# Hymba-style block on one core: the first x and weight transfers on ScalarE's queue, the selector copied on GpSimd, one block-sum transfer placed later

## The chip, the core and the metric

The kernel runs on one core of one Trainium2 chip. The metric is the device time of one execution in microseconds; of three runs of the kernel before the median is 900.09 us (900.05 to 902.27). A core has five engines with instruction queues of their own: TensorE (PE, matmuls and weight loads), VectorE (DVE), ScalarE (ACT), GpSimd (POOL) and SyncE (SP, which here only issues transfers). They wait for each other through semaphores. Transfers (DMAs) are issued by an instruction on SyncE's, ScalarE's or GpSimd's queue and carried out by 16 DMA engines beside them.

## The reference, cut to what matters

One layer: an adaLN modulation from the vector c, an RMS norm of x, one wide input projection, dilated window attention over 16 heads beside gated linear attention over 4 heads, an output projection, a residual and a final norm.

```python
mod = jax.nn.silu(c) @ w_cond[layer] + b_cond[layer]
shift, scale, gate = jnp.split(mod, 3, axis=-1)
h = rms_norm(x) * (1.0 + scale[:, None]) + shift[:, None]
proj = h @ w_in[layer]
...
y = jnp.concatenate([a_out, g_out], axis=-1) @ w_out[layer]
x = x + gate[:, None] * y
return rms_norm(x) * final_gain
```

All is float32 with x of 512 x 2048 and weights of 2048 x 7200 (in) and 2048 x 2048 (out). The kernel computes each float32 product as three faster ones of a high and a low part (high x high, high x low, low x high), so every operand is first split: ScalarE (sometimes VectorE) writes the rounded high part, VectorE the remainder.

## The kernel before, in words

**The start.** `scale` and `shift` are sums over c, computed on VectorE: each of the 16 row blocks k of the transposed conditioning weights (tile `cb`, 128 x 2048) is multiplied with silu(c) (tile `sb`, the same in all partitions) and reduced to one column. To have silu(c) in all 128 partitions, c comes as 4 rows of 512 (`cin`), with a selector matrix beside it (`cin[:, 512:]`, ones and zeros). The selector is copied into `sel` in the matmul's number format, c is split into `ch` and `cl` (`c_hi`, `c_lo` in the trace), and for each of the four quarters j two matmuls (`pc`, in `spread`) spread row j over the partitions; ScalarE then applies silu into `sb`.

For row block 0 the reduction is done in pieces to begin early. `cond_load(0, 0)` fetches `cb0` as four transfers in the order of `FIRST_COND`: columns 0 to 511, the last quarter (whose share of the sum TensorE takes, tile `psv`, with `scol`), then the second and the third quarter. Three reductions on VectorE use the first three quarters of `sb`; a last small addition gives `scale`. From it and x's first block (`xt0`) ScalarE makes `h_hi`, VectorE `h_lo`; with the split first weight block (`rawa0`, fetched in two halves by `half_load`) TensorE begins the projection (`sta`, line 613).

TensorE's program is written out in order: two warm matmuls of 256 columns and four of 512 on a tile of ones, the `pc` matmuls of quarters 0 to 2, `psv`, the `pc` of quarter 3, seven more warm matmuls, then `sta`. The later row blocks of this first stage are ordered by `_plan`, a small planner with estimated durations; the code before it, `small_inputs()` to `warm(7)`, is in the order in which it is written. SyncE's queue holds nearly all transfers in one order; a transfer there waits for the semaphore that an earlier one used, which is eight transfers back, and for the buffer that it fills.

**The value unit and the block sums.** The projections that follow are units of 8 weight groups with 64 ticks (a tick is three matmuls on one tile). The value projection (`values_unit`) and the output projection use Strassen-like products of half blocks, 7 instead of 8. The value unit has 28 groups, V0 to V27, of 4 ticks, 112 ticks in all. Sums of weight blocks that such products need (T1 to T4) are made in DRAM by transfers on GpSimd's queue: one copies a block (`sum_start`), a second adds another block to it on the way (`sum_add`). They are handed out over the units by `SUM_OPS_IN`; `block_sums(name)` places the n of a unit at (q + 0.5) / n of it, and `paced` makes each wait for the split of a weight group on ScalarE that was issued last at that point. The value unit has nine of them, (V, 0) to (V, 8), for the output projection. The token sums S1 to S4 that the value products need come back from DRAM by SyncE (`rawS`, line 1394) and are split into `vS` (lines 1400 and 1401).

Of the kernel before, what the change touches and what calls it, by code (L numbers as in the profile page):

```python
# [13 lines left out]
AF = mybir.ActivationFunctionType  # L14
# [179 lines left out]
def block_kernel(ctx: ExitStack, tc: tile.TileContext, a: dict):  # L194
    nc = tc.nc
# [14 lines left out]
    def T2(name, dt=F32, parts=P):  # L210
        return t2.tile([parts, 512], dt, tag="t2", name=name)

    def B8(name, shape, dt=F32):
        return b8.tile([P] + shape, dt, tag="b8", name=name)
# [10 lines left out]
    act = nc.scalar.activation  # L225
# [17 lines left out]
    cin = B8("cin", [1024])[:4]  # L243
# [3 lines left out]
    def small_inputs():  # L247
        nc.sync.dma_start(cin, a["c"])
        nc.scalar.dma_start(bcond, a["bcond"])
# [4 lines left out]
    def cond_load(k, e):  # L254

        cb = B8(f"cb{k}_{e}", [2048])
        src = a["wm"][k, e]
        for c in (slice(0, 2048),) if e or k > 1 else SECOND_COND if k else FIRST_COND:
            n = c.stop - c.start
            nc.sync.dma_start(cb[:, c], bass.AP(src.tensor, src.offset + P * c.start, [[n, P], [1, n]]))  # L260
        cond_tiles[k, e] = cb

    def RAW(name, shape):
        return wp.tile([P] + shape, F32, tag="raw", bufs=4, name=name)

    start_w = {}
# [7 lines left out]

    xt = [B8(f"xt{i}", [4, 512]) for i in range(4)]

    def x_load(k):
        nc.sync.dma_start(xt[k // 4][:, k % 4, :], a["xt"][:, k, :])

    def half_load(z):  # L280
        if not z:
            start_w["a", 0] = RAW("rawa0", [1024])
        c = slice(512 * z, 512 * z + 512)
        nc.sync.dma_start(start_w["a", 0][:, c], a["w_sa"][0, :, 0, c])

    sb = sbp.tile([P, 2048], F32, tag="sb", name="sb")
    hot = T2("hot", F32R)
# [4 lines left out]
    sel, ch, cl = (T2(n, F32R) for n in ("sel", "c_hi", "c_lo"))  # L292
# [4 lines left out]
    def warm(n, c=512):  # L297

        for _ in range(n):
            mm(psw[:, :c], hot[:, :P], hot[:, :c], start=True, stop=True)  # L300

    def spread(j, t, first):
        mm(pcs[j], sel[:, P * j:P * j + P], t, start=first, stop=not first)

    def spread_silu(j):
        act(sb[:, 512 * j:512 * j + 512], pcs[j], AF.Silu)  # L306

    with tc.manual_schedule(engines=PLANNED):
        small_inputs()
        cond_load(0, 0)  # L310
        half_load(0)
        x_load(0)
        half_load(1)
        nc.scalar.preload_act_table_set("silu_and_others")
        nc.vector.memset(hot[:, :256].bitcast(F32), 1.0)
        nc.vector.memset(hot[:, 256:].bitcast(F32), 1.0)
        nc.vector.memset(epst, EPS)
        nc.vector.memset(ch.bitcast(F32), 0.0)
        nc.vector.memset(sel.bitcast(F32), 0.0)
        nc.gpsimd.memset(cl.bitcast(F32), 0.0)  # L320
        warm(2, 256)
        warm(4)

        nc.vector.tensor_copy(ch[:4], cin[:, :512])
        act(sel[:4], cin[:, 512:], AF.Copy)
        act(scol, bcond[:, 48:], AF.Silu)
        tt(cl[:4], cin[:, :512], ch[:4].bitcast(F32), op=ALU.subtract)

        nc.vector.tensor_scalar(bcond[:, 16:32], bcond[:, 16:32], 1.0, None, op0=ALU.add)
        for j in range(4):  # L330
            if j == 3:
                for t in range(4):
                    mm(psv[:, :P], cond_tiles[0, 0][:, 1536 + P * t:1536 + P * t + P], scol[:, t:t + 1].broadcast_to([P, P]),
                       start=t == 0, stop=t == 3)
            spread(j, ch, True)
            spread(j, cl, False)
            if j < 3:
                spread_silu(j)
        warm(7)
# [133 lines left out]
    def block_sums(name):  # L473
        n = SUM_OPS_IN[name]
        r = [sum_ops.pop(0) for _ in range(n)]
        return [((q + 0.5) / n, x) for q, x in enumerate(r)]

    def whole(i):
        if i in second:
# [180 lines left out]
    for i, (st, k) in enumerate(sets[1:], 1):  # L660
        e = "ab".index(st)
        task(("load", k, e), "DMA", 3.1, [], 1000 - 200 * e - 10 * k, lambda k=k, e=e: cond_load(k, e), "b8")
        if st == "a":
            task(("x", k), "DMA", 0.78, [], 999 - 10 * k, lambda k=k: x_load(k))
        task(("w", st, k), "DMA", 1.55, [("w",) + sets[i - 1]] if i > 3 else [],
             (998.5 if st == "a" else 1000.5) - 200 * e - 10 * k,
             lambda st=st, k=k: start_load(st, k), "raw")
# [12 lines left out]
    for z in range(2):  # L680
        c = slice(512 * z, 512 * z + 512)
# [33 lines left out]
    n = len(chain) // 2  # L715
# [4 lines left out]
    for k in range(3):  # L720
        high, low_ = (("wh", "a", 2),) * 2 if k == 2 else (("wh%d" % k, 0), ("wh%d" % k, 1)), (("wl", "a", 2),) * 2 if k == 2 else (("wl%d" % k, 0), ("wl%d" % k, 1))
        for z in range(2):
            for e in (0, 2, 1):
                name = ("mm", "a", k, 7) if (z, e) == (1, 1) else ("m", k, z, e)
# [3 lines left out]
    for i in range(n):  # L728
        if i > 23:
            mm_task(i)  # L730
        st, k, j = chain[i]
# [14 lines left out]
    for i in range(n, 2 * n):  # L746
        mm_task(i)
        st, k, j = chain[i]
# [451 lines left out]

    def unit(name, natural, side=(), lr=None):
        side = sorted(spill + list(side) + block_sums(name), key=lambda x: x[0])
        spill[:] = [(at - 1, go) for at, go in side if at >= 1]
        side = [x for x in side if x[0] < 1]
# [208 lines left out]
    def values_unit(side):  # L1413
        n_groups = 4 * len(VAL_ORDER)
        for p, n in enumerate(VAL_ORDER):
            if n in ("P7", "P6", "P5", "P3"):
                name = {"P7": "S3", "P6": "S2", "P5": "S1", "P3": "S4"}[n]
                for z in range(2):
                    q = 4 * p + 2 * z
                    side.append((max(q - 6, 0.1) / n_groups, s_load(name, z)))  # L1420
                    side.append(((q - 1.9) / n_groups, s_parts(name, z)))
        side = sorted([(x * 4 / 7, go) for x, go in spill] + side + block_sums("V"), key=lambda x: x[0])
        spill[:] = [(at - 1, go) for at, go in side if at >= 1]
        side = [x for x in side if x[0] < 1]
# [342 lines left out]
    for pair, (l, r) in enumerate(OUT_PAIRS):  # L1767
# [44 lines left out]
        for z in range(2):  # L1812
            c0, t = 256 * z, slice(P, 2 * P)
            for k in range(8):
                wh, wl = wts[gi["O", (pair * len(OUT_ORDER) + OUT_ORDER.index("P2")) * 4 + k // 2]]
                c = slice(512 * (k % 2) + c0, 512 * (k % 2) + c0 + 256)
# [79 lines left out]
```

## Time and profile before

| what | value |
|---|---|
| median of three runs | 900.09 us |
| profiled execution, its own time | 900.5 us |
| its span (first to last instruction) | 898.7 us |
| TensorE busy | 889.6 us, 99% |
| VectorE busy | 732.1 us, 81% |
| ScalarE busy | 501.2 us, 56% |
| GpSimd busy | 127.1 us, 14% |
| DMA moved | 242.34 MB, mean 270 GB/s |

The profile is of one execution. In the timeline a row is: start, duration, engine, line, operation, tile written <- tiles read, shapes, and in brackets how long the engine was idle before it and what released it. PEld is the loading of weights into TensorE, PE the matmul. SPq, ACTq and POOL rows with DMA_DIRECT2D are the issuing instructions, not the transfers. In the view by stretches the columns are, after the mean TensorE clock: busy time of PE, PEld, DVE, ACT and POOL (with the number of instructions), granted clock, DMA share and GB/s. In the view of one tile a row gives minimum, median and maximum duration in ns and the first and last start in us. An engine named behind `<-` can be wrong where an instruction waits for several things: it is the one that came last by the semaphores that the profile shows.

### The profile page before, as it was taken

The page shows a single profiled execution, that of the slowest core. Times are in us where ns is not written, and L with a number is a line of the kernel's source. Part 1 is how long each engine was busy: PE and PEld are TensorE (multiplying, and loading weights), DVE is VectorE, ACT ScalarE, POOL GpSimd, SP SyncE. Part 2 cuts the span into 40 slices and gives each one's busy share as a digit, 9 for nine tenths or more (in the row PEclk, how much of TensorE's full clock was granted, in tenths as well). Part 3 has the DMA queues.
Part 4 walks back from the last instruction along what each step waited for, and adds up shares of the span by engine and source line. Part 5 has one row for each costly group of instructions (what it writes and reads, how often), then busy time and mean ns, then how long its engine had stood idle before and what let it go on. Part 6 is the DMA issues. An engine that isn't in the chain of part 4 may idle for free.

```text
span 898.7 us, 12390 instructions
## 1 busy us (share of the span) xinstructions
PE 889.6 (99%) x4193; PEld 742.1 (83%) x4193; DVE 732.1 (81%) x1225; ACT 501.2 (56%) x859; POOL 127.1 (14%) x225
## 2 busy tenths in 40 slices
PE   9999999999999999999999999999999999999996
PEld 7888788888888888888878888888888888888885
DVE  7999699877989999889668677595775759997787
ACT  5663533465756755755767544463644447555464
POOL 0000100023423233233100102111020100000001
PEclk9999999999999999999999999999999999999999
DMA  9999579597798898898878879678787898877853
GB/s 351 401 412 415 231 283 358 164 277 212 207 262 275 225 279 262 235 319 232 261 253 263 302 207 306 202 256 261 229 274 219 254 308 309 271 302 255 308 206 144
DMA packets 65417, 242.34 MB, mean 270 GB/s; under 512 B 8805, under 2 KB 11141, under 8 KB 55881
## 3 DMA queue, kind: packets, MB, share of 16 engines
q1 hardware_dynamic: 58442, 199.24, 61.6%
q0 software_dynamic: 6624, 42.02, 19.7%
q8 instruction: 33, 0.54, 0.2%
q10 hardware_dynamic: 288, 0.29, 0.1%
q14 instruction: 30, 0.25, 0.1%
HBM read 224.65 MB, written 51.47 MB: 307 GB/s over the span
## 4 chain that ended last, share of the span: by engine, by line
PE 97%; DMA 1%; DVE 1%; ACT 1%; issue 0%; ACTq 0%; DVEq 0%
PE ps_qk L232 5%; PE ps_qk L234 5%; PE ps_qk L233 5%; PE g L234 4%; PE g L232 4%; PE g L233 4%; PE ps_gg L232 3%; PE ps_ag L232 3%; PE ps_ag L234 3%; PE ps_gg L233 3%; PE ps_ag L233 3%; PE stb L234 3%; PE stb L232 3%; PE ps_gg L234 3%; PE stb L233 3%; PE o L957 3%
## 5 line engine op out<-in xcount | busy, mean ns | idle before, releaser
L892 POOL TENSOR_SCALAR p<-p,st 128x32 f32<-128x32 f32 (+2 forms) x108 | 57.5, 541 | 160.4 <-DVE st L882 105.9
L343 DVE CUSTOM_DVE_ANT_0 cb<-cb,sb,c_bcond 128x2048 f32<-128x2048 f32 (+2 forms) x32 | 73.1, 2283 | 1.6 <-ACT sb L306 1.4
L879 ACT ACTIVATE p<-p,st 128x416 f32<-128x416 f32 x64 | 41.1, 641 | 54.1 <-DVE st L875 46.6
L444 POOL DMA_DIRECT2D T<-in_w_o x32 | 23.1, 724 | 156.3 <-ACT V2h L509 12.3
L915 ACT ACTIVATE pth<-t 128x384 fp32r<-128x384 f32 x64 | 30.9, 483 | 14.8 <-PE t L909 9.6
L916 DVE TENSOR_TENSOR ptl<-t,pth 128x384 fp32r<-128x384 f32 x64 | 35.2, 550 | 3.2 <-ACT pth L915 2.2
L909 PE MATMUL t<-c_ident,p 128*128 128x128 f32 x192 | 31.3, 272 | 0.0
L909 PEld LDWEIGHTS t<-c_ident,p 128*128 128x128 f32 x192 | 24.3, 139 | 7.8
L875 DVE CUSTOM_DVE_ANT_0 p<-s,g,st 128x256 f32<-128x256 f32 x64 | 27.7, 433 | 1.9
L875 DVE CUSTOM_DVE_ANT_0 p<-s,g 128x160 f32<-128x160 f32 x64 | 23.5, 367 | 5.0 <-PE s L868 4.7
L1626 POOL TENSOR_SCALAR x<-x,rn 128x512 f32<-128x512 f32 x2 | 2.9, 1444 | 146.0 <-ACT rn L1615 142.1
L343 DVE CUSTOM_DVE_ANT_0 rawg<-rawg,crow,gate 128x1024 f32<-128x1024 f32 x16 | 20.4, 1278 | 3.1 <-DMA rawg<-in_wg 3.1
L868 PE MATMUL s<-ks,ql 128*128 128x416 f32 x64 | 22.5, 352 | 0.0
L867 PE MATMUL s<-ks,qh 128*128 128x416 f32 x64 | 22.5, 351 | 0.0
L1133 ACT ACTIVATE sq<-st,sc 128x256 f32<-128x256 f32 x24 | 12.1, 505 | 17.9 <-DVE st L1128 8.9
L938 ACT ACTIVATE pth<-g 32x128 fp32r<-32x128 f32 x64 | 19.7, 308 | 1.5
L343 DVE CUSTOM_DVE_ANT_0 rawg<-rawg,crow,c_bcond 128x1024 f32<-128x1024 f32 x16 | 20.3, 1279 | 0.2 <-DVE g L1070 0.2
L553 ACT ACTIVATE h_hi<-xt,scale 128x512 fp32r<-128x512 f32 (+1 forms) x18 | 12.7, 713 | 13.7 <-DVE scale L343 12.2
L444 POOL DMA_DIRECT2D T<-T x16 | 9.1, 571 | 78.2 <-ACT V8h L509 13.0
L1401 DVE TENSOR_TENSOR vS<-rawS,vS 128x1024 fp32r<-128x1024 f32 x8 | 9.7, 1223 | 10.1 <-ACT vS L1400 10.0
L444 POOL DMA_DIRECT2D T3V<-in_w_gv x8 | 5.6, 695 | 86.0 <-ACT qk21h L509 79.5
L587 ACT ACTIVATE h_hi<-xt,shift 128x512 fp32r<-128x512 f32 x16 | 11.5, 720 | 8.7 <-DVE shift L343 7.9
(1681 smaller groups left out, 3176.2 us busy)
## 6 DMA issues: line engine op xcount, KB each, us to landing
cb<-in_wm SPq DMA_DIRECT2D x30, 1024.0 KB, 9.3
T<-in_w_o POOLq DMA_DIRECT2D x32, 512.0 KB, 5.6
rawg<-in_wg SPq DMA_DIRECT2D x32, 512.0 KB, 6.1
raw_O<-in_w_o SPq DMA_DIRECT2D x32, 512.0 KB, 5.2
raw_qk<-in_w_qk SPq DMA_DIRECT2D x24, 512.0 KB, 4.3
raw_O<-T SPq DMA_DIRECT2D x24, 512.0 KB, 4.6
rawb<-in_w_sb SPq DMA_DIRECT2D x16, 512.0 KB, 8.1
rawv<-in_wv SPq DMA_DIRECT2D x16, 512.0 KB, 6.0
```

Of the source, the lines that this page charges most:

```text
L232: mm(ps, lh, rh, start=first, stop=False, skip_group_check=more)
L233: mm(ps, ll, rh, start=False, stop=False, skip_group_check=more)
L234: mm(ps, lh, rl, start=False, stop=last, skip_group_check=more)
L343: return nc.vector.tensor_tensor_reduce(out=w, in0=w, in1=with_, op0=ALU.mult, op1=ALU.add, scale=1.0, scalar=init, accum_out=dst)
L444: move = nc.gpsimd.dma_start(dst, src, max_dma_last_dim=8192, **how).ins
L875: top = nc.vector.tensor_tensor_reduce(out=t[:, lo:hi], in0=ps[:, lo:hi], in1=gt[h][:, at:at + 2 * (hi - lo) - 1:2], op0=ALU.add, op1=ALU.min,
L879: act(t, t, AF.Exp, bias=st[:, 0:1], scale=-1.0, accum_out=st[:, 1:2])
L892: last["pool"] = nc.gpsimd.tensor_scalar(to, of, st[:, 2:3], 1.0, op0=ALU.mult, op1=ALU.mult).ins
L909: nc.tensor.transpose(pk[:, n_ * P:n_ * P + P], t[:, first_ + kt * P:first_ + kt * P + P], ident)
L915: act(hi, src, AF.Copy)
L916: tt(lo, src, hi.bitcast(F32), op=ALU.subtract)
L957: mm(po[:, P * a0:P * a1], vv[h // 4][:, c, h % 4, :], pt[:, at:at + (a1 - a0 - 1) * step + 1:step, :], start=n_ == z == 0, stop=False, sk ...
```

## The change

The transfers of x's first block and of the first half of the first weight block are issued by ScalarE, right behind `c_bcond`, and no longer by SyncE. The copy of the selector moves from ScalarE to GpSimd. In the value unit, the fifth block-sum transfer is placed 0.07 of the unit later.

```diff
     xt = [B8(f"xt{i}", [4, 512]) for i in range(4)]
 
-    def x_load(k):
-        nc.sync.dma_start(xt[k // 4][:, k % 4, :], a["xt"][:, k, :])
+    def x_load(k, queue=nc.sync):
+        queue.dma_start(xt[k // 4][:, k % 4, :], a["xt"][:, k, :])
 
     def half_load(z):
         if not z:
             start_w["a", 0] = RAW("rawa0", [1024])
         c = slice(512 * z, 512 * z + 512)
-        nc.sync.dma_start(start_w["a", 0][:, c], a["w_sa"][0, :, 0, c])
+        (nc.sync if z else nc.scalar).dma_start(start_w["a", 0][:, c], a["w_sa"][0, :, 0, c])
...
         small_inputs()
         cond_load(0, 0)
+        x_load(0, nc.scalar)
         half_load(0)
-        x_load(0)
         half_load(1)
...
         nc.vector.tensor_copy(ch[:4], cin[:, :512])
-        act(sel[:4], cin[:, 512:], AF.Copy)
+        nc.gpsimd.tensor_copy(sel[:4], cin[:, 512:])
         act(scol, bcond[:, 48:], AF.Silu)
...
     def block_sums(name):
         n = SUM_OPS_IN[name]
         r = [sum_ops.pop(0) for _ in range(n)]
-        return [((q + 0.5) / n, x) for q, x in enumerate(r)]
+        late = {("V", 4): 0.07}
+        return [((q + 0.5) / n + late.get((name, q), 0), x) for q, x in enumerate(r)]
```

The start of SyncE's queue, before. `cb0` is the conditioning block of row block 0, in four transfers; `rawa0` stands there twice, for its two halves, and the first `xt0` row is x's first block:

```order
L248 DMA cin_86<-in_c 4x1024
L260 DMA cb0_0_110<-in_wm 128x512 x4
L284 DMA rawa0_115<-in_w_sa 128x512
L278 DMA xt0_89<-in_xt 128x512
L284 DMA rawa0_115<-in_w_sa 128x512 [waits DMAHW0_49]
L260 DMA cb1_0_175<-in_wm 128x1024 [waits DMAHW1_49]
```

and with the change:

```order
L248 DMA cin_86<-in_c 4x1024
L260 DMA cb0_0_110<-in_wm 128x512 x4
L284 DMA rawa0_116<-in_w_sa 128x512 [waits DMAHW0_49]
L260 DMA cb1_0_175<-in_wm 128x1024 [waits DMAHW1_49]
L260 DMA cb1_0_175<-in_wm 128x1024 [waits DMAHW2_49]
L278 DMA xt0_89<-in_xt 128x512 [waits DMAHW3_49]
```

Two transfers are gone from it, so that the second half of `rawa0` and all behind it stand two places further ahead; the first `xt0` row there is now x's second block. The start of ScalarE's queue, before:

```order
L249 DMA c_bcond_87<-in_bcond 128x52
L314 ACT_TABLE_LOAD
L325 ACTIVATE sel_97<-cin_86 4x512 [waits DMAHW1_49,DVE_49]
L326 ACTIVATE scol_88<-c_bcond_87 128x4 [waits DMAHW0_49]
L306 ACTIVATE sb_93<-pc0_102 128x512 [waits PE_49]
```

and with the change:

```order
L249 DMA c_bcond_87<-in_bcond 128x52
L278 DMA xt0_89<-in_xt 128x512
L284 DMA rawa0_116<-in_w_sa 128x512
L314 ACT_TABLE_LOAD
L326 ACTIVATE scol_88<-c_bcond_87 128x4 [waits DMAHW0_49]
L306 ACTIVATE sb_93<-pc0_102 128x512 [waits PE_49]
```

The two issues stand ahead of the load of the activation table, and the copy into `sel` is gone from between the table and `scol`. On GpSimd that copy comes behind its fill of `c_lo`:

```order
L320 MEMSET c_lo_99 128x512
L325 CAST sel_97<-cin_86 4x512 [waits DMAHW1_49,DVE_49]
L604 ISA
L604 TENSOR_TENSOR sa1lo_228<-rawa1_196,sa1hi_227 128x512 [waits DMAHW4_49,Activation_49]
```

The block-sum transfer keeps its place on GpSimd's queue; only the count of ScalarE instructions that it waits for is another. VectorE's and TensorE's orders are unchanged.

## The prediction

> **What bounds the kernel now.** I read the page's busy shares first, then the chain of waits in order of time, then TensorE's own waits.
>
> ```profile
> span 898.7 us, 12390 instructions
> PE 889.6 (99%) x4193; PEld 742.1 (83%) x4193; DVE 732.1 (81%) x1225; ACT 501.2 (56%) x859; POOL 127.1 (14%) x225
> ```
>
> ```profile
> 1.19 2.50 PE warm L300 x6
> ...
> 6.57 1.12 PE psv L333 x8
> 7.69 0.47 PE pc L303 x2
> 8.16 1.60 PE warm L300 x7
> 9.76 16.37 PE sta L613 x72
> ```
>
> ```profile
> PE ps_gv_P L234 <- DVE V21l L493: 0.2, 1, 0.2
> ```
>
> TensorE is busy for all but 9.1 us, and the chain runs along it from 1.19 us. Inside the span it waits for another engine once, 0.2 us at value group 21. So a DMA or an engine that becomes faster has nothing to give; what can move the time is the start, up to about 25 us, and that one place. One more reading of the chain: six warm matmuls (2 of 256 and 4 of 512 columns, 2560) took 2.50 us, the later seven (3584 columns) 1.60 us, so TensorE runs at half speed at first and at full speed by 8.16 us.
>
> The timeline of the start shows what the first real products (`sta`) stand on:
>
> ```profile
> 2.80 0.63 ACT L325 ACTIVATE sel<-cin 4x512 fp32r<-4x512 f32 x1 [0.36 <-DMA cin<-in_c]
> ...
> 3.48 0.29 PEld L303 LDWEIGHTS pc<-c_hi,sel 128*128 128x128 f32 x1 [0.50 <-ACT sel L325]
> ...
> 4.06 0.29 PEld L303 LDWEIGHTS pc<-c_lo,sel 128*128 128x128 f32 x1 [0.29 <-DVE c_lo L327]
> ...
> 5.94 1.56 PEld L333 LDWEIGHTS psv<-scol,cb 128*128 128x128 f32 x8
> ...
> 7.31 0.75 DVE L343 CUSTOM_DVE_ANT_0 cb<-cb,sb,part 128x512 f32<-128x512 f32 x1
> ...
> 8.18 0.16 DVE L537 TENSOR_TENSOR scale<-part,psv 128x1 f32<-128x1 f32 x1
> ...
> 8.67 0.95 ACT L553 ACTIVATE h_hi<-xt,scale 128x256 fp32r<-128x256 f32 x2 [1.47 <-DVE sa0hi L597]
> ...
> 9.37 0.87 PEld L613 LDWEIGHTS sta<-sa0hi,h_hi 128*128 128x128 f32 x4
> ```
>
> The third reduction (7.31) gives `scale`, `scale` and x give `h_hi`, and `sta` needs the first half of `h_hi`, ready at 8.67 + 0.95/2 = 9.15. The seven warm matmuls stand ahead of `sta` on TensorE and let it begin at 9.37. The slack is some 0.2 us: TensorE's own order sets the start, and the data are just behind it.
>
> **The change, part by part.** First the transfers. All are 256 KB with 2 KB rows. The time to landing counts from the issue (the row's start):
>
> ```profile
> L260 SPq DMA_DIRECT2D cb<-in_wm x2: 366/396/426, 1.2 to 1.6; - x2
> DMA to landing us min/median/max: 2.7/2.9/3.1
> ```
>
> ```profile
> L260 SPq DMA_DIRECT2D cb<-in_wm x2: 432/432/432, 2.1 to 2.5; - x2
> DMA to landing us min/median/max: 3.7/4.1/4.5
> ```
>
> ```profile
> L278 SPq DMA_DIRECT2D xt<-in_xt x1: 432/432/432, 3.5 to 3.5; - x1
> DMA to landing us min/median/max: 5.1/5.1/5.1
> ```
>
> ```profile
> 3.00:4.00 1.00, 1.00 (x3) 0.29 (x1) 0.90 (x3) 0.52 (x2) 0.00 (x0) 1.00 1.04 338
> ```
>
> The four pieces of `cb0` land at 1.2+2.7 = 3.9, 1.6+3.1 = 4.7, 2.1+3.7 = 5.8 and 2.5+4.5 = 7.0, x at 3.5+5.1 = 8.6. The stretch from 3 to 4 us has a DMA share of 1.04 (the column before the GB/s): the 16 engines are full, and each piece adds about a microsecond, (8.6-3.9)/5 = 0.94 with the weight half between. h_hi's 8.67 stands right behind x's landing at 8.6, although the view names `sa0hi`: x is the last piece now.
>
> The change issues x and the first weight half on ScalarE's queue, behind `c_bcond`, at about 1.15 and 1.55 us (an issue takes some 0.4 us, the 432 ns of these rows), that is beside the first two pieces of `cb0` and ahead of the third and fourth, instead of behind all four. The same six transfers fill the same engines, so the last still lands near 8.6, but it is the fourth piece of `cb0`, which the third reduction needs. That reduction then starts at 8.65 instead of 7.31, 1.34 later; `h_hi`, which then waits for `scale` alone, follows it 0.3 sooner than now (8.67 against 8.18 + 0.16 = 8.34). So `h_hi` is 1.34 - 0.3 = 1.0 late, less the slack of 0.2: `sta` starts **0.9 us later** (rounded up, as VectorE's own delay is the 1.1 of the next step). Bounds: 0, if ScalarE's two transfers wait behind SP's four; 1.3, if nothing of it is absorbed. An earlier start is excluded by the seven warm matmuls. The second piece, which `psv` needs at 5.94, gets the fourth place at worst (7.0), a pause of 1.1 us on TensorE that lies under the same delay.
>
> Here the Trainium skill speaks against the change: DMA: Bandwidth & Descriptors, "Issuing engines are not separate DMA queues", says that transfers of all issuing engines run on the same 16 DMA engines and interleave, and that a second issuer saves only issue time. The full shares above agree with it; by that rule the 0.9 stands, and if two queues were two paths it would be 0.
>
> Does the delay stay? The next steps are as tight:
>
> ```profile
> 16.31 3.10 DVE L343 CUSTOM_DVE_ANT_0 cb<-cb,sb,c_bcond 128x2048 f32<-128x2048 f32 x1 [0.20 <-DMA cb<-in_wm]
> ...
> 19.45 0.77 ACT L553 ACTIVATE h_hi<-xt,scale 128x512 fp32r<-128x512 f32 x1 [0.16 <-DVE scale L343]
> ...
> 20.27 0.88 PEld L613 LDWEIGHTS sta<-sa2hi,h_hi 128*128 128x128 f32 x4
> ```
>
> `h_hi` of the third row block ends at 20.22 and is loaded at 20.27, and VectorE has only 0.20 us of idle time ahead of it at 16.31. VectorE comes to that stage 1.1 late (its `sa0lo` pieces and `h_lo` follow the late `scale` without the pause for `h_hi` that they have now), less the 0.20: 0.9 again. TensorE has no later pauses that would give it back, so 0.9 goes to the end.
>
> Next GpSimd's copy of the selector. No row has a 4x512 copy there; the nearest are:
>
> ```profile
> L603 POOL TENSOR_TENSOR sa1lo<-rawa,sa1hi 128x512 fp32r<-128x512 f32 x1 | 1.5, 1508 | 14.5 <-ACT sa1hi L599 14.5
> L1659 POOL TENSOR_SCALAR x<-x,rn 128x512 f32<-128x512 f32 x1 | 1.0, 989 | 10.0 <-ACT rn L1615 10.0
> L320 POOL MEMSET c_lo<- 128x512 f32 x1 | 0.5, 524 | 0.3 <-POOLq L1884 0.3
> ```
>
> Between the fill, 0.52, and the two-input operation, 1.51; I take 0.7, one input lying nearer the fill. That is 0.07 later than ScalarE's 0.63, and the product with `c_lo` waits for VectorE until 4.06 anyway, so it costs nothing: the first product begins at 3.48 + 0.29 and takes 0.43 at half speed, ending 0.15 before `c_lo`'s load ends at 4.35. At 1.51 it would be 0.7 late, still under the 0.9. Gain below nothing is excluded by the same wait for `c_lo`. The removed ScalarE work frees 0.63 us for two issues of 0.4 and moves the table load (1.28) to 2.0 to 3.3 us; `scol` behind it is read at 5.94: free.
>
> Last the block sum. The fifth of nine in the value unit, the addition that completes the third T3 block of the output weights, comes at 0.57 instead of 0.5 of 112 ticks, 63.8 against 56, so it waits for ScalarE's split of group 16 instead of 14. Nothing passes it on GpSimd's queue. Around it:
>
> ```profile
> 480.18 0.80 POOL L444 DMA_DIRECT2D T<-in_w_o  x1 [8.71 <-ACT V14h L509]
> ```
>
> ```profile
> 485.53 1.05 ACT L509 ACTIVATE V16h<-raw_V 128x1024 fp32r<-128x1024 f32 x1
> ```
>
> ```profile
> 487.87 0.32 SPq L1394 DMA_DIRECT2D rawS<-S  x1
> ...
> 494.70 0.32 SPq L1394 DMA_DIRECT2D rawS<-S  x1
> ```
>
> ```profile
> 501.45 1.23 DVE L1401 TENSOR_TENSOR vS<-rawS,vS 128x1024 fp32r<-128x1024 f32 x1 [4.26 <-ACT vS L1400]
> 502.59 1.22 DVE L493 TENSOR_TENSOR V21l<-raw_V,V21h 128x1024 fp32r<-128x1024 f32 x1
> ```
>
> ```profile
> L444 POOL DMA_DIRECT2D T<-in_w_o x1: 785/785/785, 448.2 to 448.2; - x1
> ```
>
> ```profile
> L403 SPq DMA_DIRECT2D raw_V<-T3V x1: 319/319/319, 449.2 to 449.2; - x1
> ...
> DMA to landing us min/median/max: 5.5/5.5/5.5
> ```
>
> ```profile
> L403 SPq DMA_DIRECT2D raw_V<-T4V x1: 319/319/319, 475.7 to 475.7; - x1
> ...
> DMA to landing us min/median/max: 3.5/3.5/3.5
> ```
>
> It will be issued at 485.53 + 1.05 = 486.6, 1.2 us ahead of the token-sum load at 487.87. That load frees the buffer for the one at 494.70, whose splits `vS` stand ahead of V21 on ScalarE and VectorE: the one place where TensorE waits. A load issued 1 us behind such an addition (at 448.2) landed after 5.5 us, one without it after 3.5. So the cost is at most 2.0; the gain at most 0.3, if the wait for V21 goes (its load had the old addition's backlog ahead). I take **0.5**, nearer to the low end, as the four loads behind 481 us lose the backlog that they have now.
>
> **The sum.** The profiled execution took 900.5 us (span 898.7 and 1.8 around it): 900.5 + 0.9 + 0 + 0.5 = 901.9. It stood 0.4 above the median of the runs, 900.09, so the forecast for the median is **901.5 us**, 0.16% slower, which a measurement of this kernel (0.3%, 2.7 us) can't tell from no change.
>
> **Rivals.** *Nothing reaches TensorE*, 900.1 (899.8 to 900.6): the pieces on SP's queue are served in time and the addition falls in a gap. For it: 0.2 us of slack exists, and group 21's stall may go. Against: full DMA engines from 3 us.
>
> *The clock stays low*, slower. Place: `psv`, where TensorE pauses up to 1.1 us. At half speed it ran from 1.19 to at least 6.57, 5.4 us. If the pause starts that anew at 7.0, half speed lasts to 12.4, and `psv` (1.12, mostly at half speed now), the last `pc` (0.47 doubled) and the seven warm matmuls (1.60 doubled) take 5.3 from there and end near 12.3 instead of 9.4: 2.9 later, with the 0.5 of the block sum 903.5. It decides once the half speed lasts beyond about 11.6. Against: the waits at 3.48 and 4.06 did no visible harm. The Trainium skill, TensorE: Matmul & The Clock Gate, "Part 1", says that full speed follows one busy window of about 3.4 us that runs freely; this too can delay it by a window, and no row here shows the window.
>
> *A slow first copy on GpSimd.* Whatever the copy takes beyond about 1.8 us (0.78 until `c_lo` is waited for anyway, and the 0.9) delays everything one for one. The first two-input operation there took 1.51; 3.1 us, twice that, gives 902.8, and no row has such a cost. The Trainium skill, GPSIMD Engine Reference, "Instruction dispatch", names some 6 us for the first call of freshly loaded code, by which it would be 905.
>
> **How the numbers follow.** Forecast 0.52, nothing 0.32, clock 0.11, slow copy 0.05. Range 899.8 to 903.5: from the second case's low end to the clock's price. Slower than 902.8: most of the last two and a tail of the first, where the bounds 1.3 and 2.0 meet, 0.17; below 897.4 only by a gain that a busy TensorE has no room for, 0.03; within, 0.80.
>
> **What would show it.** In the new profile: the fourth piece of `cb0` landing past 8 us and the third reduction released by a DMA; a wait ahead of `psv`; `sta` at 10.2 to 10.4; GpSimd's copy of 0.5 to 1.0 us; the addition issued at V16h, and V21 waited for longer than 0.2. It is wrong if `sta` starts before 9.6, if ScalarE's transfers land after SP's four pieces, or if V21's wait is gone.

## The result and the profile after

Over 18 runs of each, the changed kernel has a median of 902.94 us (900.94 to 905.82), the kernel before 900.12 us (899.75 to 902.27): a ratio of 1.0031, with a 95% interval of 1.0023 to 1.0039. So it is slower by 0.31%, a small loss whose interval does not reach 1, and it scatters over 4.9 us where the kernel before stays within 2.5. The profiled execution took 905.61 us, one of the longest of the 18, 5.1 us more than the 900.5 of the profile before: it shows a long run and not the median.

TensorE's waits (what waits, for whom; us in all, times, longest; the 1.2 us before the first warm matmul, the same in both, left out):

```profile
PE ps_gv_P L232 <- ACT V19h L510: 0.9, 1, 0.9
PE ps_gv_P L234 <- DVE V19l L494: 0.7, 1, 0.7
PE sta L614 <- ACT h_hi L554: 0.4, 1, 0.4
PE psv L333 <- DMA cb<-in_wm: 0.2, 1, 0.2
```

Before, the only such wait behind the first warm matmul was 0.2 us at value group 21. That one is gone, but nothing can be read from it: it is gone from the profiles of E1, E3, E4 and E11 below too, whose value unit is that of before. Two places are new: the start (`psv`, `sta`) and value group **19**.

The timeline of the start:

```profile
2.77 0.85 POOL L325 CAST sel<-cin 4x512 fp32r<-4x512 f32 x1 [1.50 <-DMA cin<-in_c]
...
8.28 0.75 DVE L343 CUSTOM_DVE_ANT_0 cb<-cb,sb,part 128x512 f32<-128x512 f32 x1 [1.24 <-DMA cb<-in_wm]
...
9.17 0.75 DVE L343 CUSTOM_DVE_ANT_0 cb<-cb,sb,part 128x512 f32<-128x512 f32 x1
...
10.22 0.95 ACT L554 ACTIVATE h_hi<-xt,scale 128x256 fp32r<-128x256 f32 x2 [2.87 <-DVE scale L538]
...
10.79 0.76 PEld L614 LDWEIGHTS sta<-sa0hi,h_hi 128*128 128x128 f32 x4 [0.83 <-ACT h_hi L554]
```

The reductions on VectorE wait for pieces of `cb0` until 8.28 us, `h_hi` now waits for `scale`, and the first real product begins at 10.79 instead of 9.37, 1.42 later.

The other place. First ScalarE before, around the token sum's split `vS`, then the same two rows in the changed kernel, then its token-sum load with the time to landing:

```profile
492.35 1.06 ACT L1400 ACTIVATE vS<-rawS 128x1024 fp32r<-128x1024 f32 x1 [1.57 <-DMA rawS<-S]
493.32 1.04 ACT L509 ACTIVATE V19h<-raw_V 128x1024 fp32r<-128x1024 f32 x1
```

```profile
498.17 1.06 ACT L1401 ACTIVATE vS<-rawS 128x1024 fp32r<-128x1024 f32 x1 [5.81 <-DMA rawS<-S]
499.13 1.04 ACT L510 ACTIVATE V19h<-raw_V 128x1024 fp32r<-128x1024 f32 x1
```

```profile
L1395 SPq DMA_DIRECT2D rawS<-S x1: 319/319/319, 489.4 to 489.4; - x1
...
DMA to landing us min/median/max: 8.7/8.7/8.7
```

`vS` stands ahead of V19's split in ScalarE's queue. Its load lands after 8.7 us instead of 4.5 (487.87 to 492.3 before), ScalarE stands idle for 5.81 us, and V19, whose own data have long been there, is split late. What TensorE then does, in stretches (after the mean clock columns as before: PE, PEld, DVE, ACT, POOL, granted clock, DMA share, GB/s):

```profile
498.00:500.00 2.00, 1.36 (x7) 0.78 (x5) 0.74 (x1) 1.83 (x2) 0.00 (x0) 1.00 0.73 295
500.00:502.00 2.00, 1.06 (x3) 0.59 (x4) 2.00 (x3) 1.49 (x3) 0.00 (x0) 1.00 0.24 82
502.00:504.00 2.00, 2.00 (x7) 1.57 (x6) 0.75 (x1) 0.02 (x1) 0.00 (x0) 0.61 0.90 299
504.00:506.00 2.00, 2.00 (x6) 1.55 (x6) 0.93 (x1) 2.00 (x3) 0.00 (x0) 0.54 0.91 324
506.00:508.00 2.00, 2.00 (x11) 1.60 (x10) 2.00 (x4) 0.93 (x1) 0.79 (x1) 1.00 0.59 199
```

Behind the two pauses of 0.9 and 0.7 us the mean granted clock of two stretches is 0.61 and 0.54 (in stretches of half a microsecond it is 0.50 from 502.5 to 505.5). TensorE is "busy" all that time, but at that clock it does in 4 us what else takes 2.3: 2 x 0.39 + 2 x 0.46 = 1.7 us are lost without any wait that the view of waits would name.

The 5.1 us of this execution are then: start 1.4, pauses at group 19 1.6, low clock 1.7, which makes 4.7; the rest is not placed.

As far as the mean clocks of the runs show, the low clock belongs to this one execution. Its mean granted clock over the whole span is 0.995; the other 17 runs of the changed kernel have 0.997 to 0.999, like the kernel before, and among them are those of 905.82 and 904.82 us (both 0.998). So the clock doesn't make the loss of the median nor most of the scatter. What the other long runs lose is then probably waits of TensorE, longer than the 1.6 us seen here; none of them was profiled, so this is not shown.

### The profile page after: what moved, and what is told of

It reads as the page before. It is cut to its first block, busy times and chain, and to the rows that moved or that the text cites. A ratio compares the mean times of both kernels' runs of the same rounds, so it can differ in the third digit from the quotient of the medians.

```text
span 903.8 us, 12391 instructions
## 1 busy us (share of the span) xinstructions
PE 892.7 (99%) x4193; PEld 742.6 (82%) x4193; DVE 732.6 (81%) x1225; ACT 499.9 (55%) x858; POOL 127.9 (14%) x226
## 4 chain that ended last, share of the span: by engine, by line
PE 96%; DMA 1%; DVE 1%; ACT 1%; issue 0%; ACTq 0%; DVEq 0%
PE ps_qk L232 5%; PE ps_qk L234 5%; PE ps_qk L233 5%; PE g L234 4%; PE g L233 4%; PE g L232 4%; PE ps_gg L232 3%; PE ps_ag L232 3%; PE ps_gg L234 3%; PE ps_ag L233 3%; PE ps_ag L234 3%; PE stb L234 3%; PE stb L233 3%; PE ps_gg L233 3%; PE stb L232 3%; PE o L958 3%
```

## The experiments

Each has 11 or 12 runs (E7 six), beside the kernel before on the same chip. Times are medians in us, in brackets the lowest and highest run; the ratio, with its interval, is not the quotient of the two medians.

| | kernel | time | before | ratio (95%) |
|---|---|---|---|---|
| E1 | start edits alone | 901.03 (900.38 to 902.51) | 900.15 | 1.0007 (0.9999 to 1.0016) |
| E2 | late block sum alone | 901.74 (900.46 to 906.68) | 900.15 | 1.0025 (1.0011 to 1.0039) |
| E3 | selector on GpSimd alone | 900.21 (899.67 to 901.01) | 900.15 | 1.0001 (0.9993 to 1.0010) |
| E4 | queue move alone | 900.92 (900.62 to 902.03) | 900.15 | 1.0008 (1.0000 to 1.0017) |
| E5 | E2, next copy late too | 900.55 (899.72 to 902.17) | 900.25 | 1.0004 (0.9995 to 1.0012) |
| E6 | block sum early | 900.18 (899.74 to 901.31) | 900.25 | 1.0002 (0.9993 to 1.0010) |
| E7 | block sum 0.09 late | 905.42 (902.20 to 910.28) | 900.25 | 1.0063 (1.0041 to 1.0086) |
| E8 | E2, a copy for the addition | 900.44 (899.68 to 901.01) | 900.25 | 0.9999 (0.9991 to 1.0008) |
| E9 | E2, token sum split later | 900.48 (899.63 to 901.07) | 900.21 | 0.9999 (0.9990 to 1.0008) |
| E10 | token sum split later alone | 900.27 (899.78 to 900.88) | 900.21 | 1.0001 (0.9992 to 1.0010) |
| E11 | x alone on ScalarE's queue | 900.25 (899.79 to 901.58) | 900.21 | 0.9999 (0.9990 to 1.0008) |
| E12 | whole change and E10 | 901.09 (900.46 to 901.72) | 900.21 | 1.0008 (0.9999 to 1.0017) |

### Which edit costs (E1 to E4)

E1 is the change without the late block sum (the diff is against the change):

```diff
-        late = {("V", 4): 0.07}
-        return [((q + 0.5) / n + late.get((name, q), 0), x) for q, x in enumerate(r)]
+        return [((q + 0.5) / n, x) for q, x in enumerate(r)]
```

> The two start edits alone (x and the first weight half on ScalarE's queue, the selector on GpSimd), the block sum where it was. Theory A (the fourth conditioning piece becomes the last transfer in every run): the first real product at 10.5 to 10.9 us instead of 9.37, no wait at value groups 19 to 21 beyond the old 0.2, 901.3 to 901.8 in every run with a spread under 1.5 us. Rival B (the start varies from run to run, and the 900.9 to 905.8 of the whole change come from it): a median near 902.5 with a spread of several us. Rival C (the start is hidden in most runs): 900.1.

Measured: 901.03, 0.88 more than before, within 2.1 us (theory A had 1.5; all runs but one lie within 0.9). The third and fourth piece of `cb0` (issued at 2.1 and 2.5), the last two reductions and the first real product:

```profile
L260 SPq DMA_DIRECT2D cb<-in_wm x2: 432/437/442, 2.1 to 2.5; - x2
...
DMA to landing us min/median/max: 5.5/5.6/5.7
```

```profile
7.67 0.75 DVE L343 CUSTOM_DVE_ANT_0 cb<-cb,sb,part 128x512 f32<-128x512 f32 x1 [1.16 <-DMA cb<-in_wm]
...
8.56 0.75 DVE L343 CUSTOM_DVE_ANT_0 cb<-cb,sb,part 128x512 f32<-128x512 f32 x1
...
9.43 0.16 DVE L537 TENSOR_TENSOR scale<-part,psv 128x1 f32<-128x1 f32 x1
...
9.62 0.95 ACT L553 ACTIVATE h_hi<-xt,scale 128x256 fp32r<-128x256 f32 x2 [2.19 <-DVE scale L537]
...
10.20 0.76 PEld L613 LDWEIGHTS sta<-sa0hi,h_hi 128*128 128x128 f32 x4 [0.56 <-ACT h_hi L553]
```

The third piece lands at 2.1 + 5.5 = 7.6 instead of 5.8, the fourth at 2.5 + 5.7 = 8.2 instead of 7.0. It is the third that sets the time: the second reduction waits for it until 7.67 (6.42 before, 1.25 later), and the third reduction follows at 8.56 without a wait, its piece being there. So `scale` is 1.25 later than before (9.43 against 8.18), `h_hi` 0.95 and `sta` 0.83. The time lies a little below theory A's, since the start is 0.6 better here than in the profiled run of the whole change; rivals B and C are out. The interval of the ratio alone just reaches 1; what makes the loss sure is that three kernels with this queue move, E1, E4 and E12, give 0.88, 0.77 and 0.88.

E2 is the kernel before with the three lines of the diff on the block sum.

> The late block sum alone, the start as it was. Theory A (the addition, issued 1 us ahead of the token-sum load and 4 us ahead of the next copy, makes the loads behind it late by an amount that differs from run to run): waits of 0 to 2 us at value groups 19 to 21, a clock below 1 behind them where they are long, median 901.0 to 902.0 and a spread of 3 us or more. Rival B (the spread belongs to the start): 900.1 to 900.6 with a spread under 1.5 us.

Measured: 901.74, but the twelve runs lie apart: five from 900.46 to 900.83, three at 901.7 to 902.0, four from 904.23 to 906.68. So the scatter of the whole change belongs to this edit, and it costs 0.3 to 0.7 us in five runs, 1.6 to 1.8 in three and 4 to 6.5 in four. Here the mean granted clock is 0.994 or 0.995 in three of the four long runs and 0.998 in the other. The profiled run took 904.23 (0.995); its waits at group 19, and its token-sum load:

```profile
PE ps_gv_P L232 <- ACT V19h L510: 1.2, 1, 1.2
PE ps_gv_P L234 <- DVE V19l L494: 0.7, 1, 0.7
```

```profile
L1395 SPq DMA_DIRECT2D rawS<-S x1: 320/320/320, 488.0 to 488.0; - x1
...
DMA to landing us min/median/max: 9.0/9.0/9.0
```

E3 and E4 part the start edits. E3:

```diff
-        act(sel[:4], cin[:, 512:], AF.Copy)
+        nc.gpsimd.tensor_copy(sel[:4], cin[:, 512:])
```

> The selector's copy on GpSimd alone, the queues as they were. Theory: the copy takes 0.85 us as in the changed kernel, the first spread product comes 0.2 later and the following ones 0.1 to 0.2 later, which the seven warm matmuls pass on: 900.1 to 900.4. Rival (the late start of the changed kernel comes from this copy): the first real product past 10 us and 901.3 or more.

E4 is E1 with the selector's copy left on ScalarE:

```diff
-        nc.gpsimd.tensor_copy(sel[:4], cin[:, 512:])
+        act(sel[:4], cin[:, 512:], AF.Copy)
```

> The two issues on ScalarE's queue alone, the selector copied by ScalarE, behind the activation-table load, which the issues put off. Theory A (the order of landing sets the start): the third reduction past 9 us, the first real product at 10.4 to 10.9, 901.1 to 901.8. ScalarE's copy comes at about 3.45 to 4.1, so the first spread product 0.6 later than now, hidden under the same delay. Rival: as the selector sets the start, 900.7 (the 0.6 alone).

Measured: E3 0.06 more than before, E4 0.77 more, with `sta` at 10.23 (its second reduction waits until 7.71 and its third comes at 8.60, not past 9; the pieces landed after 5.5 and 5.7 us, as in E1). The copy on GpSimd costs nothing that can be measured; the queue move has the start's 0.8 to 0.9 to itself. That ScalarE's `sel` came 0.6 later in E4 added nothing, as expected.

### What makes the token-sum load late (E5 to E8)

E5 keeps the block sum late and puts the next one, a copy inside DRAM, as much later:

```diff
-        late = {("V", 4): 0.07}
+        late = {("V", 4): 0.07, ("V", 5): 0.07}
```

> The fifth block-sum transfer 0.07 later as in the change, and the sixth (a copy inside DRAM, 3.7 us behind it in the changed kernel) 0.07 later too, behind the split of group 20 instead of 18; the start as before. Theory A (the addition stands 1 us ahead of the token-sum load, which lands 4 us later, and the token sum's split stands ahead of V19 on ScalarE): the waits at V19 stay in some of the runs, median 901.0 to 902.5, spread of 3 us or more. Rival B (the addition is squeezed against the next copy, and the two together hold up the loads): with the old spacing the waits go, 900.1 to 900.6 with a spread under 1.5 us.

Measured: 900.55, which is rival B's number, though over 2.5 us; and the waits at group 19 are still there in the profiled run (901.71, one of the longer ones), as theory A had it:

```profile
PE ps_gv_P L234 <- DVE V19l L494: 0.7, 1, 0.7
PE ps_gv_P L232 <- ACT V19h L510: 0.4, 1, 0.4
```

```profile
L1395 SPq DMA_DIRECT2D rawS<-S x1: 320/320/320, 487.4 to 487.4; - x1
...
DMA to landing us min/median/max: 8.2/8.2/8.2
```

The addition alone makes the load late. Whether the copy behind it makes it later still is not shown: the load lands after 8.2 us here, and with the copy close behind after 7.4 (E9) to 9.0 (E2); only the missing runs above 902.2 speak for it. Three profiles give one rule for the price: landing time less the 4.5 of before less the waits at group 19 is 8.7 - 4.5 - 1.6 = 2.6 in the changed kernel, 9.0 - 4.5 - 1.9 = 2.6 in E2, 8.2 - 4.5 - 1.1 = 2.6 in E5. So in these TensorE loses nothing until the load takes 7.1 us, then one for one. The low clock came behind waits of 1.6 and 1.9 us and not behind 1.1: in E5 the clock stayed at 1.00. That is no threshold, since E7 below has 1.7 us of waits at a clock of 1.00. Neither theory alone is right.

E6 goes the other way:

```diff
-        late = {("V", 4): 0.07}
+        late = {("V", 4): -0.07}
```

> The fifth block-sum transfer 0.07 earlier than before, so behind the split of group 13 instead of 14: about 478.1 us instead of 480.2, 7 us behind the copy ahead of it. Theory A: the token-sum load at 479.8 is now the one that stands behind the addition, by 1.7 us. It may land 4 us later (487 to 488.8 instead of 484); its split and V17 behind it have 1.9 us of slack, so 0 to 0.5 is lost, or nothing; the loads behind come sooner and the 0.35 us wait at V21 can go: 899.7 to 900.5. Rival (any place 1 to 2 us ahead of a token-sum load costs the same): 901 or more with a spread of 3 us.

Measured: 900.18, no wait in the value unit. The addition now stands 1.8 us ahead of an earlier token-sum load and costs nothing there. The wait at group 21 of before is gone, as it is where the value unit was not touched, and the median gains nothing that could be told from noise.

E7 puts it a little later yet, behind the token-sum load:

```diff
-        late = {("V", 4): 0.07}
+        late = {("V", 4): 0.09}
```

> The fifth block-sum transfer 0.09 later instead of 0.07, behind the split of group 17: issued at 488.5 to 489, some 0.7 us behind the token-sum load at 487.9 and 2 us ahead of the next copy. Theory A: that load lands as before (4.5 us), no wait at V19; what it holds up now are the loads of V21 to V23 and the next token-sum load, so a wait at V21 of 0 to 1.5 us: 900.1 to 901.6. Rival B (the nearness to the next copy costs): as with 0.07 or worse, waits at V19, 901.7 or more with runs past 904.

Measured: 905.42 over six runs, none below 902.20, one at 910.28: much worse, as rival B had it. But the place is theory A's. In its shortest run, the profiled one:

```profile
PE ps_gv_P L232 <- ACT V21h L510: 1.0, 1, 1.0
PE ps_gv_P L234 <- DVE V21l L494: 0.7, 1, 0.7
```

```profile
L1395 SPq DMA_DIRECT2D rawS<-S x2: 320/320/320, 487.8 to 493.8; - x2
...
DMA to landing us min/median/max: 3.6/3.6/3.6
```

```profile
L1395 SPq DMA_DIRECT2D rawS<-S x1: 320/320/320, 493.8 to 493.8; - x1
...
  ACT vS L1401: 6.2, 1
```

The load ahead of the addition lands in 3.6 us and group 19 doesn't wait. The next token-sum load (493.8) is the late one: ScalarE waits 6.2 us for it (4.4 before), and group 21, which waited 0.2 us before, waits 1.7. The clock stays at 1.00 in this run. In the four runs of 904 to 910 us it did not: their mean granted clock is 0.993 to 0.996, against 0.998 and 0.999 in the two shorter ones. A thousandth of 900 us is 0.9 us, so the clock is some 2 to 5 us of their loss by estimate; where it fell was not profiled.

E8 is E2 with that one transfer as a plain copy; the addition of a quarter of one T3 block of the output weights is left out:

```diff
-            paced(dsum[pair, name, g], flat(block(pair, BLOCK_SUMS[name][1], g)), accum_op=ALU.add)
+            how = {} if (pair, name, g) == (0, "T3", 2) else {"accum_op": ALU.add}
+            paced(dsum[pair, name, g], flat(block(pair, BLOCK_SUMS[name][1], g)), **how)
```

> As with the late block sum alone, but that transfer copies its block instead of adding it (the addition of one quarter of one T3 block of the output weights is left out). Theory A1 (it is the addition, which also reads what stands in DRAM, that fills the DMA engines): the token-sum load lands after 5 to 6 us, no waits at V19, 900.1 to 900.6. Theory A2 (any transfer of 512 KB 1 us ahead does it): as with the addition, 901.7 and a spread of 3 us or more.

Measured: 900.44, no waits at group 19. The transfer in E2 and in E8, then the token-sum load of E8:

```profile
L444 POOL DMA_DIRECT2D T<-in_w_o x1: 800/800/800, 487.0 to 487.0; - x1
...
DMA to landing us min/median/max: 8.4/8.4/8.4
```

```profile
L444 POOL DMA_DIRECT2D T<-in_w_o x1: 501/501/501, 487.1 to 487.1; - x1
...
DMA to landing us min/median/max: 5.3/5.3/5.3
```

```profile
L1396 SPq DMA_DIRECT2D rawS<-S x2: 320/320/320, 488.1 to 495.9; - x2
...
DMA to landing us min/median/max: 5.4/5.4/5.4
```

The same 512 KB at the same place land after 5.3 us as a copy and after 8.4 as an addition, and the load 1 us behind takes 5.4 instead of 9.0. So A1: it is the addition that makes the load late. The stretch behind it, E2 first, E8 below:

```profile
488.00:492.00 4.00, 4.00 (x20) 3.27 (x19) 3.50 (x3) 2.94 (x5) 0.51 (x1) 1.00 0.86 154
```

```profile
488.00:492.00 4.00, 4.00 (x20) 3.30 (x19) 3.60 (x4) 3.03 (x5) 0.50 (x1) 1.00 0.92 304
```

The DMA engines are nearly as busy (0.86 against 0.92) and move half as much by the count of this view, 154 GB/s against 304. What they do in the rest of the time no row shows.

### Taking the load off ScalarE's path (E9, E10, E12), and half a queue move (E11)

The second S1 token sum is needed by group 22, yet its split stands ahead of V19's. E9 puts it behind that of group 21 on ScalarE (its low part on VectorE then comes behind that group's too), with the block sum late as in E2:

```diff
-            act(t[:, 0, :], s_raw[n, z], AF.Copy)
+            with tc.issue_after(last["hi"]) if (n, z) == ("S1", 1) else nullcontext():
+                act(t[:, 0, :], s_raw[n, z], AF.Copy)
```

> The late block sum alone, and the split of the second S1 token sum (needed by group 22) put behind the split of group 21 on ScalarE instead of ahead of that of group 19. The load still stands 1 us behind the addition. Theory A (the late landing costs only because that split stands ahead of V19): the token-sum load still lands after 8 to 9 us, V19 to V21 no longer wait for it, 899.7 to 900.4 with a spread under 1.5 us; the 0.35 us wait of before at V21 goes too. Rival C (the weight loads behind the addition are late themselves): waits at V20 to V22 instead, 900.8 to 902.

Measured: 900.48 within 1.4 us, ratio 0.9999. The load takes 7.4 us in the profiled run, less than the 8 to 9 expected, and ScalarE doesn't wait for it ahead of V19:

```profile
L1395 SPq DMA_DIRECT2D rawS<-S x2: 320/320/320, 488.4 to 494.7; - x2
...
DMA to landing us min/median/max: 7.4/7.4/7.4
```

```profile
492.35 1.06 ACT L510 ACTIVATE V19h<-raw_V 128x1024 fp32r<-128x1024 f32 x1 [1.02 <-PE ps_gv_P L233]
...
498.36 1.06 ACT L510 ACTIVATE V21h<-raw_V 128x1024 fp32r<-128x1024 f32 x1 [1.88 <-PE ps_gv_P L234]
499.33 1.05 ACT L1402 ACTIVATE vS<-rawS 128x1024 fp32r<-128x1024 f32 x1
```

(A row of two loads gives the landing of the first, here as in E7 and E8.) V19 is split at 492.35, V21 at 498.36, and what ScalarE waits for there is TensorE. No group from 19 to 22 waits. By the rule above 7.4 us would have cost only 0.3 in the old order, so this profile alone proves little; the eleven runs, none above 901.07 where seven of E2's twelve lie above 901.7, speak for theory A. E10 is the same move on the kernel before, E12 on the whole change.

> The same move of the token sum's split without the late block sum. Theory A: nothing is late, the 0.35 us wait at V21 goes: 899.6 to 900.1, the start as before. Rival C (the next token-sum load, whose buffer now comes free 4 us later, holds up V22 and the loads behind it): a wait at V22 of 0.3 or more, 900.3 to 901.

> The whole change with the token sum's split moved behind that of group 21. Theory A: the part that belongs to the block sum goes, the start's stays: 900.6 to 901.2 with a spread under 2.5 us. Rival C: 901.7 or more.

Measured: E10 900.27, nothing gained over before; E12 901.09 (900.46 to 901.72), as good as E1's 901.03. E12's profile is the clear case: its load is as late as E2's, which by the rule would cost 1.9, and no value group waits.

```profile
L1395 SPq DMA_DIRECT2D rawS<-S x1: 319/319/319, 489.2 to 489.2; - x1
...
DMA to landing us min/median/max: 9.0/9.0/9.0
```

The move takes away what the block sum costs and its scatter, and leaves the start's 0.9. No kernel tried is faster than the one before.

E11 puts x alone on ScalarE's queue, with the selector on ScalarE and the block sum as before (the diff is against E4):

```diff
-        (nc.sync if z else nc.scalar).dma_start(start_w["a", 0][:, c], a["w_sa"][0, :, 0, c])
+        nc.sync.dma_start(start_w["a", 0][:, c], a["w_sa"][0, :, 0, c])
```

> x alone on ScalarE's queue, the first weight half on SyncE's behind the four conditioning pieces, the selector on ScalarE, the block sum as before. Theory A (each transfer put ahead of the fourth piece delays it by what it takes of the full DMA engines): the fourth piece lands near 7.9 instead of 7.0, the weight half near 8.6, the first real product at 9.6 to 9.8 instead of 9.37, 900.3 to 900.6, less than half of what both cost (0.8 to 0.9). The selector's copy comes 0.2 us later, behind the table load, hidden as before. Rival D (an issue on ScalarE's queue costs as such, by the table load and the copy that it puts off): as both, 900.8 to 901.1.

Measured: 900.25, 0.04 over before. The third and fourth piece of `cb0`, and the first product:

```profile
L260 SPq DMA_DIRECT2D cb<-in_wm x2: 438/440/441, 2.1 to 2.5; - x2
DMA to landing us min/median/max: 4.4/4.6/4.9
```

```profile
9.29 0.87 PEld L613 LDWEIGHTS sta<-sa0hi,h_hi 128*128 128x128 f32 x4
```

With one transfer ahead of it the fourth piece lands at 2.5 + 4.9 = 7.4, 0.4 later than before, the third reduction starts 0.3 later, and `sta` starts when TensorE's own order lets it. An issue on ScalarE's queue costs nothing that can be measured (D is out), and I had priced one transfer too high: here it is the second that is paid for.

## Why the prediction was right or wrong

**The place and size of the start, right, one step wrong.** Forecast 0.9; E1 measured 0.88, E4 0.77. The order of landing sets the start, as forecast: `scale` is 1.25 late (1.34 forecast), `h_hi` 0.95 and waits for `scale` alone (1.0), `sta` at 10.20 (10.2 to 10.4 forecast). In the profiled run of the whole change `sta` was 1.42 late, over the upper bound of 1.3: the third and fourth piece landed after 6.1 and 6.3 us there and after 5.5 and 5.7 in E1. The step that was wrong: not the fourth piece but the third makes the delay, 1.8 us late (7.6 instead of 5.8), and the wait is the second reduction's. That this gives the third reduction at 8.56, where the fourth piece's forecast landing gave 8.65, is luck. By the Trainium skill, DMA: Bandwidth & Descriptors, "Issuing engines are not separate DMA queues", the two queues share the same engines; E1 and E4 agree with it: what ScalarE's queue issues makes the pieces on SyncE's land 1.2 to 1.8 us later.

**The delay stays to the end, right.** E1's token-sum load is issued 0.7 later than before (488.6 against 487.9) and its span is 0.7 us longer (899.4 against 898.7), of 0.83 at the first product.

**The selector, right.** The copy took 0.85 us (0.7 forecast) and cost nothing: E3.

**The block sum, mis-sized, and its place missed.** The term was 0.5, its bounds -0.3 and 2.0. Alone it costs 1.6 in the median (E2), inside the bounds, and up to 6.5 in a run. Three steps of it failed.

First the landing. I took the 5.5 us of the load 1 us behind the addition at 448.2 for the worst; here the same distance gave 7.4 to 9.0. The profile before had a nearer row: the addition that is moved stood at 480.2 and landed after 7.9 us, and the load 1.3 us behind it took 7.5:

```profile
raw_V<-T1V SPq DMA_DIRECT2D x1, 512.0 KB, 7.5
```

With 7.5 for 5.5 the upper bound would have been 4.0. Second the place: I followed the late load to the buffer that it frees, and so to group 21, and did not look at what stands behind its split on ScalarE, although the same timeline has V19 right behind `vS`. E9 and E12 show that this order carries the loss; group 21, whose longer wait was to be the sign, does not wait at all in the changed kernel, which the prediction itself names as a sign of being wrong. Third the slack: ahead of V19 it is 2.6 us, which I did not have. A landing 4.5 us late (E2) less 2.6 makes 1.9, close to the bound of 2.0: that the median lies within is luck, two errors that offset each other. "Nearer to the low end" had no ground, since the other end was not an end, and the gain of 0.3 rested on a wait at group 21 that comes and goes by itself.

**The rivals.** *The clock stays low* was named at `psv`, where the pause was 0.2 us and did no harm; in E12 it was 0.6 us and did none either. The clock did fall, by 1.7 us of work, in the profiled run at the stall that I had not placed; by their mean clocks it did not in the other runs of the change. *Nothing reaches TensorE* is nearly what five runs of E2 show for the block sum alone; it does not hold for the start, where the four profiles with the queue move have `sta` at 10.20 to 10.79. The *slow copy* did not happen: 0.85 us. Its sums were loose: twice 1.51 is 3.0, and 6 us by the same sum would give 905.7, not 905.

**The number.** 901.5 was forecast and 902.94 measured, 1.4 too low, within the range of 899.8 to 903.5: a loss of 2.8 us where 1.4 was forecast, that is the start's 0.9 as forecast and 1.9 instead of 0.5 for the rest. The range reached so far up because of the clock at `psv`, which did not happen. Within 0.3% was given 0.80, slower 0.17; the median is 0.1 us past that boundary of 902.8, and the interval (0.23 to 0.39%) lies on both sides of it. That single runs would scatter by 5 us was not foreseen: eight of the 18 lie above 903.5.

## What to carry to other kernels

When a transfer is moved, look for the load that it now stands ahead of, and then at everything behind that load's consumer in its engine's queue: the first victim is whatever stands next in order there, even if its own data are ready and the load is wanted much later. An operation that is needed late should not stand early in a queue if it waits for memory; E12 made a load that comes 4.5 us late free by moving one split. Before a transfer is moved, read what it did to the load behind it where it stands now: that row was nearer than the one I used. And where the margin is a threshold, as here some 7.1 us of landing, a median hides it: look at the scatter of the runs before calling two places equal.

## What was not expected of the hardware

- A transfer that adds to what stands in DRAM landed after 8.4 us where a copy of the same 512 KB took 5.3, and in the 4 us behind it the engines moved 154 GB/s at a busy share of 0.86 (E2). Elsewhere an addition landed after 5.2 us (448.2 in the kernel before). Its issue on GpSimd took 0.80 us instead of 0.50.
- Behind two pauses of TensorE, 0.9 and 0.7 us within some 3 us, the granted clock was 0.50 for about 3 us, which doubled the price of the stall in that run; behind 1.2 and 0.7 in E2 it was the same. In E7's profiled run pauses of 1.0 and 0.7 did not do it, nor 0.4 and 0.7 in E5's. The Trainium skill, TensorE: Matmul & The Clock Gate, "Part 1", has the clock fall after an idle window of about 3.4 us and calls this window free-running. In these two profiles less idle time than that was enough; whether the same pauses can hit or miss a window, these runs do not show.
- The start of one and the same program differs between executions. In the nine profiles with the queues of before `sta` begins anywhere from 8.86 (E5) to 10.02 us (E6, where x landed after 5.9 us instead of 5.1); in the four with the queue move from 10.20 to 10.79. So the start of one profile against one other says little below a microsecond.
